# A decoder layer with dilated attention: attention keys stored in three orders, joined loads, and later value and gate products

## The chip, the core and the metric

The kernel runs on one core of a Trainium2 chip. A core has a matrix engine (TensorE, here PE, with its weight loads shown apart as PEld), a vector engine (DVE), a scalar engine (ACT), a third elementwise engine (POOL, also called GpSimd), and an engine (SP) that mostly issues transfers. Sixteen DMA engines move data between DRAM and the on-chip memory of 128 partitions. Matmul results land in PSUM, eight banks of 128 x 512 floats. The metric is the time of one execution on the device in microseconds (us), from the first to the last work of the core; lower is better.

## What is computed

One layer for a sequence of 2048 positions and width 1024, all in float32:

```python
h = rms_norm(x, norm1_g)
q, k, v, u, g = split(h @ w_in)                 # each 512 wide
q, k = rms_norm per head of 64 (8 heads)
a = dilated_attention(q, k, v)                  # branches (window, dilation) = (128,1), (512,4), (2048,16)
m = gelu(u) * (W_s @ layer_norm(gelu(g)) + b)   # chunks of 128 positions, 4 groups, W_s lower triangular
x = x + concat(rms_norm(a), rms_norm(m)) @ w_out
x = x + square(relu(rms_norm(x) @ w_ff1)) @ w_ff2
```

In each attention branch a query at t attends the keys t, t - d, t - 2d, ... down to t - window (d the dilation), that is up to 129 keys among the positions of its residue modulo d. The three branches are combined with weights from their softmax denominators, so a single maximum per query and head over all branches, one sum of exponentials and one weighted sum of values suffice.

## The kernel before

Numbers are split in two parts, a rounded high one and the remainder, so that fast matmuls give float32 accuracy: a product is the sum of high x high, high x low and low x high (`gemm3`, L215; 24 matmuls of 512 columns for a 128 x 512 block of a projection over 1024 inputs). The stages follow one another:

1. **First sweep** (`sweep1`, L340). For each of 16 tiles of 128 positions it computes the q, k and v products (loop L550; c = 0, 1, 2), normalizes q and k, and, one tile behind (`behind`, L509), transposes them to 64 dimensions by positions, two heads to a 128-partition block (`pr` counts the four head pairs), and splits them. Four tiles make a group G. The keys go to DRAM in the order of positions (`kt_d`, L141; `store_t`, L413). The queries go there in the order of their residue modulo 16 (`qt_d`; `store_q`, L420, which first copies each block on ACT (high part) or POOL (low part) and then issues one transfer per half of the partitions). In between, the maxima of branches 1 and 4 are found from the scores of the high parts (`max1`, `max4`, `maxima`, L443 to L492). After the last tile's keys the gate products g of tiles 14 and 15 are made and kept in DRAM (`ge_d`, L578), and then the last maxima. Part of these are done in `finish` (L598), which runs inside the attention's set-up.

2. **Attention** (`attention`, L610). Here every engine's instructions keep the order in which they are written (`InOrder`, L64). For a head, `prepare` (L624) loads `ks` (128 rows: the 64 dimensions' high parts, then their low parts), `qh` (the queries' high part twice), `k2` (the keys' high part and a row of ones, 65 rows) and `q2` (the queries' low part and a row of negated maxima), six transfers of 64 partitions each. The score of a block of 128 keys is then two matmuls with keys as weights:

```python
pe.matmul(ps[:, n : n + w], ks, qh, start=True, stop=False)      # (k high + k low) . q high
pe.matmul(ps[:, n : n + w], k2, q2, start=False, stop=True)      # k high . q low, minus the maximum
```

   A head has 20 jobs: eight for branch 1 (two key blocks each), then for each of four residues r two jobs of branch 4 (two blocks each) and one of branch 16 (four blocks). In branch 1 the keys of a block adjoin; in branch 4 the weights are every fourth key (L831), in branch 16 every sixteenth (L837). A job's scores get the mask added on DVE, two exponentials on ACT (a rounded one and a full one), the difference of the two on POOL (or on DVE, for the jobs in `LODS`), and four jobs later (`PD`) its value matmuls (`pv`, L740; three per block). After the jobs in `MXAT`, four 64-row matmuls and DVE maxima (`group`, L656) find branch 16's maxima for the next head, with its keys at stride 16 as the moving operand. SP issues all loads of the next head at the head's start, values at the jobs `V1AT` and `V4AT`.

3. **Second sweep** (`sweep2`, L923): per tile the products u and g (`gemm_g`, L970, skipped for tiles 14 and 15), the gating (`mixer`, `gate`), the output projection.

4. **MLP** (`mlp`, L1153): by a seven-product scheme of 2 x 2 blocks; the last half of the time.

Outside the attention a scheduler that estimates times orders each engine's instructions, with those written earlier going first among the ones that are ready. Transfers issued by one engine start in the order of its queue, and an instruction that waits holds up those behind it.

Of the kernel before, what the change touches and what calls it, by code (L numbers as in the profile page):

```python
# [8 lines left out]
F32 = mybir.dt.float32  # L9
F32R = mybir.dt.float32r  # L10
# [20 lines left out]
PD, PB, EB, LOL, EVL = 4, 5, 4, 2, 1  # L31
# [4 lines left out]
MXAT = (5, 8, 11, 14)  # L36
V1AT, V4AT = 12, 4
# [3 lines left out]
GEAT = 13  # L41
# [19 lines left out]
PSB, MXB, HS0 = 4, 1, 0  # L61

# [41 lines left out]
def tile_hybrid_block(  # L104
# [35 lines left out]
    qt_d = dram.tile([H, P, S], F32, name="qt_d")  # L140
    kt_d = dram.tile([H, P, S], F32, name="kt_d")  # L141
# [4 lines left out]
    ge_d = dram.tile([2, P, GW], F32, name="ge_d")  # L146
# [169 lines left out]

    mk1 = mkp_pool.tile([P, 2, 256], F32, name="mk1")
# [6 lines left out]
    def masks(m):  # L324

        mk = mkp_pool.tile([P, 384], F32, name=f"mk{m}")
# [7 lines left out]
    m4t, m4e = masks(4)  # L334
    m16t, m16e = masks(16)
# [4 lines left out]
    def sweep1():  # L340
        if True:
# [8 lines left out]
            wh = [zh] + [[wp.tile([P, AW], F32R, name=f"wh{c}_{k}") for k in range(KD)] for c in (1, 2)]  # L350
            wl = [zl] + [[wp.tile([P, AW], F32R, name=f"wl{c}_{k}") for k in range(KD)] for c in (1, 2)]
# [61 lines left out]
            def store_t(dst, part, src, toks):  # L413
                for hh in range(2):
                    nc.sync.dma_start(
                        dst[hh::2, part * HD : (part + 1) * HD, toks].rearrange("h d t -> d h t"),
                        f32(src[hh * HD : (hh + 1) * HD]),
                    )

            def store_q(G):  # L420

                for pr in range(NG):
                    for part, src in ((0, f32(qhis[G])), (1, qlos[G])):
                        src = src[:, pr, :].rearrange("p (i s) -> p s i", s=16)
                        end = G == NT // 4 - 1
                        tag = "qn" if part == 0 and end else "qp"
                        queue = nc.scalar if part == 1 and end else nc.sync
                        qp = sp.tile([P, AW], F32, tag=tag, name="qp", bufs=2).rearrange("p (s i) -> p s i", s=16)
                        if part == 0:
                            nc.scalar.activation(qp, src, AF.Copy)  # L430
                        else:
                            nc.gpsimd.tensor_copy(qp, src)  # L432
                        for hh in range(2):
                            queue.dma_start(
                                qt_d[2 * pr + hh, part * HD : (part + 1) * HD, :].rearrange("d (s i) -> d s i", s=16)[
                                    :, :, G * 32 : (G + 1) * 32
                                ],
                                qp[hh * HD : (hh + 1) * HD],
                            )
# [65 lines left out]
            qhis, qlos = {}, {}  # L505
# [3 lines left out]
            def behind(t, qn, kn, step):  # L509

                G, tg = divmod(t, 4)
                if step == 0:
                    if tg == 0:
                        qhis[G] = sp.tile([P, NG, 512], F32R, tag="qhi", name="qhi")
                        qlos[G] = sp.tile([P, NG, 512], F32, tag="qlo", name="qlo", bufs=1)
                    los["k"] = sp.tile([P, NG, P], F32R, tag="klo", name="klo")
# [4 lines left out]
                    transposed(kn, None, kring[:, :, pos * P : (pos + 1) * P], los["k"])  # L521
                    store_t(kt_d, 1, los["k"], toks)
                    if G == NT // 4 - 1:
                        store_t(kt_d, 0, kring[:, :, pos * P : (pos + 1) * P], toks)
                    elif tg == 3:
                        gt = slice(G * 512, (G + 1) * 512)
                        store_t(kt_d, 0, kring[:, :, (G % 2) * 512 : (G % 2 + 1) * 512], gt)
                    if tg == 3:
                        store_q(G)
# [17 lines left out]

            last = None
            gsrc = w_in[:, 3 * AW + GW : 3 * AW + 2 * GW]
            for t in range(NT):  # L550
# [5 lines left out]
                for c in range(3):  # L556
                    ps = psm.tile([P, AW], F32, tag="mm", name="ps_mm")
# [3 lines left out]
                    if c < 2:  # L561
                        ns.append(normed(ps, r))
                    else:
                        vt = vts[t % 2]
                        split_sb(vt[:, :, 0:HD], vt[:, :, HD + 2 : VW], ps.rearrange("p (h d) -> p h d", d=HD), r)
                        nc.sync.dma_start(v_d[:, t * P : (t + 1) * P, :].rearrange("h t c -> t h c"), f32(vt))
                    if last is not None:
                        behind(t - 1, *last, c)
                    if t == NT - 1 and c == 0:
                        wg["h"], wg["l"] = wg_tiles()  # L570
                        for k in range(KD):
                            raw = sp.tile([P, AW], F32, tag="graw", name="graw", bufs=2)
# [5 lines left out]
            for t in (NT - 2, NT - 1):  # L578
                _, xh, xl, r = xs[t]
                ps = psm.tile([P, AW], F32, tag="mm", name="ps_mm")  # L580
                gemm3(ps, [(xh[:, k, :], xl[:, k, :], wg["h"][k], wg["l"][k]) for k in range(KD)])
                ge = sp.tile([P, GW], F32, tag="graw", name="ge")
                nc.scalar.activation(ge, ps, AF.Copy, scale=r)
                nc.scalar.dma_start(ge_d[t - NT + 2], ge)
# [13 lines left out]
            def finish(pe, dve):  # L598

                order[:] = pe, dve  # L600
                yield lambda pool: load_x_t(pool, pst, 0, nxt=1)
# [8 lines left out]
    def attention(finish, xnp, xs, tpe, wu):  # L610
        with ExitStack() as st:
# [10 lines left out]
            k2s = []  # L622
# [870 lines left out]
```

## Time and profile before

| | |
|---|---|
| median of three runs | 2426.0 us (2423.41 to 2440.55) |
| profiled execution | 2441.18 us, span 2439.5 us |
| PE busy | 2357.1 us (97%) |
| first sweep up to its last keys | 0 to 378 us |
| last products, last maxima, set-up | 378 to 421 us |
| attention | 421 to 731 us |
| second sweep | 731 to about 1190 us |
| MLP | to 2439.5 us |

The profile's groups and timelines give the source line, the engine, the operation, the tiles written and read, and the shapes (for a matmul: weight rows * weight columns, then rows x columns of the moving operand). Lines in attention show as L74, the line of the ordering helper, so they are told apart by tiles: `ps_as` are scores, `ps_o` values, `ps_mx` branch 16's maxima, `ps_sc` the other maxima. Matmuls are pipelined, so their durations overlap and the distance between starts is what one costs. PEclk is the share of TensorE's full clock that was granted.

### The profile page before, as it was taken

Reading aid. Unit: us, or ns where it says so; the run is one execution under the profiler, and the core shown is the slowest. Engines: PE = TensorE matmul, PEld = TensorE weight load, DVE = VectorE, ACT = ScalarE, POOL = GpSimd, SP = SyncE. Lnnn points to the kernel's source line nnn. Section 1 sums busy time; section 2 is a strip of 40 time slices with the busy share of each in tenths; the row PEclk is TensorE's granted clock in tenths of the full one; section 3 lists DMA queues with packets and bytes.
Section 4 is the critical chain, followed back from the end, with each engine's and each line's share of the span. In section 5 each row is a group of like instructions: output and inputs, shape, how many; then the busy total and the mean of one; then the engine's idle time right before and its main releaser. Section 6 shows DMA issues by size and latency. Waiting matters only on the chain. (4 is left out here: it accounts for less than half of the span.)

```text
span 2439.5 us, 31701 instructions
## 1 busy us (share of the span) xinstructions
PE 2357.1 (97%) x11292; PEld 1958.9 (80%) x11292; DVE 1461.1 (60%) x2940; ACT 973.0 (40%) x1584; POOL 843.3 (35%) x657
## 2 busy tenths in 40 slices
PE   8999997999997999998989999999999999999999
PEld 6777775999996788886778887788878888888887
DVE  6556666565565665665775557655557566565542
ACT  5323222656673222223544555555543232222321
POOL 1000001555551122222566666667752001131210
PEclk9999997789898999998999999999999999999999
DMA  6435247656744433333666556654559665575652
GB/s 195 87 79 118 61 101 166 187 150 192 197 148 104 102 89 97 92 89 117 203 191 191 150 154 194 195 155 148 155 177 335 217 198 190 182 241 180 190 172 78
DMA packets 432301, 382.34 MB, mean 157 GB/s; under 512 B 89704, under 2 KB 358632, under 8 KB 427528
## 3 DMA queue, kind: packets, MB, share of 16 engines
q1 hardware_dynamic: 415408, 377.68, 53.1%
q10 hardware_dynamic: 16736, 2.65, 0.7%
q8 instruction: 89, 1.46, 0.3%
q14 instruction: 68, 0.56, 0.1%
HBM read 259.80 MB, written 120.39 MB: 156 GB/s over the span
## 5 line engine op out<-in xcount | busy, mean ns | idle before, releaser
L1292 PE MATMUL ps_f<-hop,wop 128*128 128x512 f32 x2688 | 620.1, 392 | 11.9 <-ACT c L1300 3.2
L1414 PE MATMUL ps_f<-split 128*128 128x512 f32 x2688 | 611.1, 390 | 2.8 <-ACT c L1279 2.8
L1292 PEld LDWEIGHTS ps_f<-hop,wop 128*128 128x128 f32 x2688 | 507.6, 189 | 122.7 <-ACT hop L188 4.3
L1414 PEld LDWEIGHTS ps_f<-split 128*128 128x128 f32 x2688 | 505.8, 188 | 108.2 <-ACT c L1279 3.2
L1204 POOL TENSOR_TENSOR as<-w1r 128x512 f32<-128x512 f32 x160 | 213.5, 1342 | 164.9 <-DVE wop L189 149.6
L188 ACT ACTIVATE split<-sr 128x1024 fp32r<-128x1024 f32 x112 | 118.4, 1060 | 330.5 <-PE ps_f L1414 325.6
L1204 POOL TENSOR_TENSOR c<-c 128x512 f32<-128x512 f32 x160 | 233.7, 1485 | 45.0 <-ACT c L1280 30.7
L1424 DVE TENSOR_TENSOR acc<-acc,ps_f 128x512 f32<-128x512 f32 x192 | 124.4, 682 | 206.1 <-PE ps_f L1414 205.9
L1204 POOL TENSOR_TENSOR raw<-raw 128x1024 f32<-128x1024 f32 x40 | 101.4, 2543 | 420.8 <-DMA raw<-in_w_ff_dram 388.6
L74 POOL TENSOR_TENSOR pl<-e,ph 128x512 fp32r<-128x512 f32 x144 | 175.6, 1231 | 154.8 <-ACT e L74 127.0
L189 DVE TENSOR_TENSOR wop<-as,wop 128x512 fp32r<-128x512 f32 x160 | 149.5, 935 | 91.3 <-ACT wop L188 88.9
L188 ACT ACTIVATE wop<-as 128x512 fp32r<-128x512 f32 x160 | 100.3, 629 | 214.0 <-POOL as L1204 128.0
L74 DVE TENSOR_TENSOR ps_as<-ps_as,mk 128x512 f32<-128x512 f32 (+1 forms) x160 | 105.7, 663 | 122.8 <-PE ps_as L74 112.9
L189 DVE TENSOR_TENSOR split<-sr,split 128x1024 fp32r<-128x1024 f32 x112 | 162.9, 1455 | 16.6 <-ACT split L188 12.0
L74 PE MATMUL ps_o<-ph,v 128*64 128x128 f32 (+3 forms) x816 | 154.0, 276 | 1.4 <-ACT nacc L74 1.4
L74 PE MATMUL ps_as<-qh,ks 128*128 128x256 f32 (+1 forms) x384 | 143.0, 378 | 0.0
L74 ACT ACTIVATE ph<-ps_as 128x512 fp32r<-128x512 f32 (+1 forms) x160 | 92.4, 577 | 126.8 <-DVE ps_as L74 126.6
L432 POOL COPY qp<-qlo 128x512 f32<-128x512 f32 x16 | 17.1, 1074 | 363.5 <-DVE qlo L411 155.3
L74 PE MATMUL ps_as<-q,k 65*128 65x256 f32 (+1 forms) x384 | 139.1, 370 | 0.0
L452 DVE CUSTOM_DVE_ANT_0 jk<-ps_sc,mk 128x256 f32<-128x256 f32 (+1 forms) x232 | 92.5, 399 | 53.3 <-PE ps_sc L448 47.2
L74 PEld LDWEIGHTS ps_o<-ph,v 128*65 128x65 f32 (+1 forms) x816 | 114.4, 157 | 1.6 <-ACT nacc L74 1.6
L74 PEld LDWEIGHTS ps_as<-qh,ks 128*128 128x128 f32 x384 | 108.0, 281 | 3.0
(262 smaller groups left out, 4080.8 us busy)
## 6 DMA issues: line engine op xcount, KB each, us to landing
s_d<-c SPq DMA_DIRECT2D x224, 256.0 KB, 2.2
sr<-s_d SPq DMA_DIRECT2D x112, 512.0 KB, 3.6
raw<-in_w_ff_dram SPq DMA_DIRECT2D x96, 512.0 KB, 4.8
w1r<-in_w_ff_dram SPq DMA_DIRECT2D x128, 256.0 KB, 3.2
v<-v_d SPq DMA_DIRECT2D x24, 1040.0 KB, 12.8
xt<-in_x_dram SPq DMA_DIRECT2D x32, 512.0 KB, 4.1
raw<-h_d SPq DMA_DIRECT2D x28, 512.0 KB, 5.5
v_d<-vt SPq DMA_DIRECT2D x16, 520.0 KB, 6.2
```

What stands on the lines that cost most here:

```text
L74: return self.tc.keep_in_program_order(op(*args, **kwargs))
L188: en.scalar.activation(dst_hi, raw, AF.Copy)
L189: (en.gpsimd if on_pool else en.vector).tensor_tensor(dst_lo, raw, f32(dst_hi), ALU.subtract)
L432: nc.gpsimd.tensor_copy(qp, src)
L452: order[1].tensor_tensor_reduce(jk[:, :n], ps[:, j, :n], mk, 1.0, -3e38, ALU.add, ALU.max, accum_out=m[:, col : col + 1])
L1204: nc.gpsimd.tensor_tensor(dst, a, b, op)
L1292: nc.tensor.matmul(ps[bank], a[:, k, :], b[k], start=first and k == n == 0, stop=(k == 3 and n == 2), skip_group_check=True,)
L1414: nc.tensor.matmul(ps, s[a][:, k, :], t[b][:, k % 2, :], start=k == m == 0, stop=k == NH - 1 and m == 2)
L1424: nc.vector.tensor_tensor(c, c, ps, op)
```

## The change

- **Three orders.** Beside `kt_d` there are now `k4_d` and `k16_d`, the keys ordered by residue modulo 4 and 16, and the queries' `qt_d`; all are laid out by head pair and part (`[NG, 2, P, S]`). `store_g` and `store_by` write them for each group of four tiles: a copy (on POOL, with one exception per order in the last group) and one transfer of 128 partitions. The keys' low parts are kept for four tiles (`klos`) and stored with one transfer a group.
- **Scores.** Branch 4 takes its weights from a tile `k4`, branch 16 from `k16`, both with the keys of a block adjoining. A block's score in these branches is three matmuls (`three`): the row of ones (one weight row) with the negated maxima, the 128 rows with `qh`, and the first 64 rows with the queries' low part. Branch 1 keeps two matmuls, with `k1` and `k2`; there is a single `k2` now. `group` takes its moving operand from `k16`, adjoining.
- **Loads.** `k16`, `k1` and `k4` are one transfer of 128 partitions each, `qh` one with its source repeated. `k4` is loaded at the head's own start, `k1` and `k2` for the next head after job 9 (`K1AT`).
- **Late products.** The value products of tiles 14 and 15 are made after the last tile's keys, and then gate products for four tiles, 14, 15, 12, 13 (`PRE`), the last two with x loaded and transposed once more; the second sweep skips its gate products for these four.
- **Last group.** Only head pair 0 is stored before the attention's set-up; the other 18 blocks are copied and stored in `finish`, through SP's ordered queue.
- **Room.** The masks of branches 4 and 16 are built at the attention's start in a tile that is used again later; `e` has 3 buffers for 4 (`EB`), DVE's share of the differences comes one job earlier (`LOL`), and `MXAT` is (6, 9, 11, 13) for (5, 8, 11, 14).

The core of the diff:

```diff
-PD, PB, EB, LOL, EVL = 4, 5, 4, 2, 1
+PD, PB, EB, LOL, EVL = 4, 5, 3, 1, 1
...
-MXAT = (5, 8, 11, 14)
-V1AT, V4AT = 12, 4
+MXAT = (6, 9, 11, 13)
+V1AT, V4AT, K1AT = 12, 4, 9
...
-GEAT = 13
+PRE = (14, 15, 12, 13)
...
+            def store_by(dst, m, G, pr, part, src, sync):
+
+                end = G == NT // 4 - 1
+                n = 512 // m
+                tag = "qn" if part == 0 and end else "qp"
+                qp = sp.tile([P, AW], F32, tag=tag, name="qp", bufs=2 if tag == "qn" else QPB).rearrange("p (s i) -> p s i", s=m)
+                src = f32(src).rearrange("p (i s) -> p s i", s=m)
+                if end and part == 0 and pr == 0:
+                    nc.scalar.activation(qp, src, AF.Copy)
+                else:
+                    nc.gpsimd.tensor_copy(qp, src)
+                if sync is None:
+                    sync = nc.scalar if part == 1 and end else nc.sync
+                sync.dma_start(dst[pr, part].rearrange("p (s i) -> p s i", s=m)[:, :, G * n : (G + 1) * n], qp)
+
+            def store_g(G, todo, sync=None):
+
+                cols = slice((G % 2) * 512, (G % 2 + 1) * 512)
+                for pr, part in todo:
+                    k, q = (klos[G][:, pr, :], qlos[G][:, pr, :]) if part else (kring[:, pr, cols], qhis[G][:, pr, :])
+                    store_by(qt_d, 16, G, pr, part, q, sync)
+                    store_by(k16_d, 16, G, pr, part, k, sync)
+                    store_by(k4_d, 4, G, pr, part, k, sync)
...
-                        store_q(G)
+                        store_g(G, [(pr, part) for part in (1, 0) for pr in range(NG)] if G < NT // 4 - 1 else ((0, 0), (0, 1)))
...
+                    if c == 2 and t >= NT - 2:
+                        behind(t - 1, *last, c)
+                        continue
...
+                gemm3(ps, [(xh[:, k, :], xl[:, k, :], wh[2][k], wl[2][k]) for k in range(KD)])
+                keep_v(t, ps, r)
+            for n, t in enumerate(PRE):
+                if t < NT - 2:
+                    xs[t] = load_x_t(xp, pst, t, newton=True)
...
-                sy.dma_start(f32(qh[0:HD, :]), qt_d[h, 0:HD, :])
-                sy.dma_start(f32(ks[0:HD, :]), kt_d[h, 0:HD, :])
-                sy.dma_start(f32(ks[HD:P, :]), kt_d[h, HD:P, :])
-                sy.dma_start(f32(q2[0:HD, :]), qt_d[h, HD:P, :])
-                sy.dma_start(f32(qh[HD:P, :]), qt_d[h, 0:HD, :])
-                sy.dma_start(f32(k2[0:HD, :]), kt_d[h, 0:HD, :])
+                both = lambda t: t[pr, :, rows, :]
+                sy.dma_start(f32(k16), both(k16_d))
+                sy.dma_start(f32(qh), qt_d[pr, 0:1, rows, :].broadcast_to([2, HD, S]))
+                sy.dma_start(f32(q2[0:HD, :]), qt_d[pr, 1, rows, :])
...
-                        pe.matmul(ps[:, j, :], qh[0:HD, s * P : (s + 1) * P], ks[0:HD, s::16], start=True, stop=True)
+                        pe.matmul(ps[:, j, :], qh[0:HD, s * P : (s + 1) * P], k16[0:HD, s * P : (s + 1) * P], start=True, stop=True)
...
-                for ks, k2, qh, q2, w in units:
-                    pe.matmul(ps[:, n : n + w], ks, qh, start=True, stop=False)
-                    pe.matmul(ps[:, n : n + w], k2, q2, start=False, stop=True)
+                for pairs, w in units:
+                    for j, (k, q) in enumerate(pairs):
+                        pe.matmul(ps[:, n : n + w], k, q, start=j == 0, stop=j == len(pairs) - 1)
                     n += w
...
+                def three(k, q, q2):
+
+                    return (ones, q2[HD : HD + 1]), (k, q), (k[0:HD], q2[0:HD])
...
-                            s0 = r + cb * 512
-                            kk, qq = slice(s0, s0 + 509, 4), slice(32 * cb, 32 * cb + n)
-                            units.append((ks[:, kk], k2[:, kk], qv[:, r, :, qq], q2v[:, r, :, qq], 4 * n))
+                            kk, qq = slice(512 * r + cb * P, 512 * r + (cb + 1) * P), slice(32 * cb, 32 * cb + n)
+                            units.append((three(k4[:, kk], qv[:, r, :, qq], q2v[:, r, :, qq]), 4 * n))
...
-                        kk, qq = slice(s, None, 16), slice(s * P, (s + 1) * P)
-                        units.append((ks[:, kk], k2[:, kk], qh[:, qq], q2[:, qq], P))
+                        kk = slice(s * P, (s + 1) * P)
+                        units.append((three(k16[:, kk], qh[:, kk], q2[:, kk]), P))
...
-                if t >= NT - 2:
+                if t in PRE:
                     return None
```

`ones` is row 64 of a tile set to 1; the negated maxima lie in row 64 of `q2`.

More of the change, by code (lines that the diff above doesn't have):

```diff
@@ L61 @@
 PSB, MXB, HS0 = 4, 1, 0
+QPB = 3
 class InOrder:
@@ L137, in tile_hybrid_block @@
     dram = ctx.enter_context(tc.tile_pool(name="dram", bufs=1, space=DRAM))
-    qt_d = dram.tile([H, P, S], F32, name="qt_d")
-    kt_d = dram.tile([H, P, S], F32, name="kt_d")
+    qt_d, kt_d, k4_d, k16_d = (dram.tile([NG, 2, P, S], F32, name=f"{n}_d") for n in ("qt", "kt", "k4", "k16"))
     v_d = dram.tile([H, S, VW], F32, name="v_d")
@@ L322, in tile_hybrid_block, with masks @@
     m16f = mk1[:, 0, 0:P].unsqueeze(1).broadcast_to([P, 4, P])
-    def masks(m):
-        mk = mkp_pool.tile([P, 384], F32, name=f"mk{m}")
+    def masks(mk, m):
         nc.gpsimd.memset(mk, 0.0)
@@ L349, in sweep1 @@
             zh, zl = wg_tiles()
-            wh = [zh] + [[wp.tile([P, AW], F32R, name=f"wh{c}_{k}") for k in range(KD)] for c in (1, 2)]
-            wl = [zl] + [[wp.tile([P, AW], F32R, name=f"wl{c}_{k}") for k in range(KD)] for c in (1, 2)]
+            wh, wl = {0: zh}, {0: zl}
+            for w, c in ((wh, 2), (wh, 1), (wl, 1), (wl, 2)):
+                w[c] = [wp.tile([P, AW], F32R, name=f"w{'h' if w is wh else 'l'}{c}_{k}") for k in range(KD)]
             vts = []
@@ L413, in store_t @@
             def store_t(dst, part, src, toks):
[L414 to L439, printed above, removed]
@@ new lines, in store_t @@
+                nc.sync.dma_start(dst[:, part, :, toks].rearrange("g p t -> p g t"), f32(src))
+            def store_by(dst, m, G, pr, part, src, sync):
[11 more added lines that the diff above has]
+                sync.dma_start(dst[pr, part].rearrange("p (s i) -> p s i", s=m)[:, :, G * n : (G + 1) * n], qp)
@@ L546, in late4, with keep_v @@
                     store_m(G, range(H))
+            def keep_v(t, ps, r):
+                vt = vts[t % 2]
+                split_sb(vt[:, :, 0:HD], vt[:, :, HD + 2 : VW], ps.rearrange("p (h d) -> p h d", d=HD), r)
+                nc.sync.dma_start(v_d[:, t * P : (t + 1) * P, :].rearrange("h t c -> t h c"), f32(vt))
             last = None
@@ L596, in sweep1, with finish @@
             st.close()
-            def finish(pe, dve):
+            def finish(pe, dve, sy):
                 order[:] = pe, dve
+                store_g(G, [(pr, part) for pr in range(1, NG) for part in (0, 1)], sy)
                 yield lambda pool: load_x_t(pool, pst, 0, nxt=1)
@@ L641, in prepare, with load_k @@
                 V = {}
-                T = [ks, qh, k2, q2, V]
+                T = [qh, q2, k16, V]
+                def load_k(m):
+                    k = first.pop(m, None)
+                    if k is None:
+                        k = (tp if m == 1 else sp).tile([P, S], F32R, tag=f"k{m}", name=f"k{m}", bufs=1)
+                    T.append(k)
+                    sy.dma_start(f32(k), both(kt_d if m == 1 else k4_d))
+                    if m == 1:
+                        sy.dma_start(f32(k2[0:HD, :]), kt_d[pr, 0, rows, :])
                 def load_v(part):
                     if part == 1:
-                        V[1] = v_tile(tp, "v1")
+                        V[1] = first.pop("v", None)
+                        if V[1] is None:
+                            V[1] = v_tile(tp, "v1")
                         sy.dma_start(f32(V[1]), v_d[h].rearrange("(b i) c -> i b c", i=P))
@@ L692, in due @@
                     f()
-            T, group, load_v = prepare(0)
+            T, group, load_v, load_k = prepare(0)
+            load_k(1)
             load_v(1)
             act.activation(root, ones_c, AF.Exp)
-            more = finish(pe, dve)
+            more = finish(pe, dve, sy)
             if X0S is None:
@@ L905, in attention @@
                         load_now(4)
+                    if h + 1 < H and i == K1AT:
+                        load_k(1)
                     if h + 1 < H and i == V1AT:
```

77 lines of the change are left out of this document (39 added, 38 removed).

## The prediction

> **What bounds the kernel now.** I read the page first, then stretches of the span, then single heads, then the matmuls of two jobs.
>
> ```profile
> PE 2357.1 (97%) x11292; PEld 1958.9 (80%) x11292; DVE 1461.1 (60%) x2940; ACT 973.0 (40%) x1584; POOL 843.3 (35%) x657
> ...
> 0.00:378.00 378.00, 370.46 (x1657) 281.35 (x1658) 232.52 (x898) 125.60 (x236) 19.06 (x34) 1.00 0.45 105
> 391.40:421.10 29.70, 19.66 (x60) 12.66 (x61) 20.10 (x101) 3.57 (x5) 1.80 (x1) 0.50 0.94 206
> 421.10:731.00 309.90, 307.06 (x2127) 299.78 (x2127) 182.87 (x459) 199.11 (x368) 177.47 (x147) 0.85 0.64 176
> 1104.00:1190.00 86.00, 73.71 (x328) 60.39 (x328) 55.55 (x111) 32.84 (x62) 21.28 (x19) 0.92 0.50 162
> ```
>
> The last four rows are stretches: start and end, length, busy time of PE, weight loads, DVE, ACT and POOL, granted clock, DMA share, GB/s. 421.10 to 731.00 is the attention, which the change rewrites. There PE works 307 of 310 us; ACT, the next, 199. So what the change does to PE there sets the result. The clock in that row is 0.85 although PE is never idle.
>
> ```profile
> 421.10:460.50 39.40, 39.40 (x232) 38.27 (x231) 19.52 (x57) 22.62 (x42) 21.61 (x18) 0.68 0.56 147
> 538.50:573.70 35.20, 35.20 (x270) 34.38 (x267) 22.34 (x61) 23.62 (x44) 21.77 (x18) 1.00 0.74 197
> ```
>
> These are heads 0 and 3. The attention's 309.9 us are 38.7 us a head; with the clock at 1.00 one takes 35.2, at 0.68 39.4.
>
> **The scores before.** Start times of consecutive matmuls give the price of each (durations overlap, so I use differences of starts).
>
> ```profile
> 559.78 0.38 PE L74 MATMUL ps_as<-qh,ks 128*128 128x128 f32 x1
> 560.00 0.39 PE L74 MATMUL ps_as<-q,k 65*128 65x128 f32 x1
> ...
> 561.58 0.22 PE L74 MATMUL ps_o<-ph,v 128*64 128x128 f32 x1
> 561.64 0.45 PE L74 MATMUL ps_as<-qh,ks 128*128 128x256 f32 x1
> 561.92 0.40 PE L74 MATMUL ps_as<-q,k 65*128 65x256 f32 x1
> 562.16 0.40 PE L74 MATMUL ps_as<-qh,ks 128*128 128x256 f32 x1
> ...
> 568.11 0.46 PE L74 MATMUL ps_as<-qh,ks 128*128 128x256 f32 x1
> ...
> 573.87 0.29 PE L74 MATMUL ps_as<-q,k 65*128 65x256 f32 x1
> 573.99 0.29 PE L74 MATMUL ps_as<-qh,ks 128*128 128x256 f32 x1
> ...
> 574.24 0.23 PE L74 MATMUL ps_o<-ph,v 128*65 128x128 f32 x1
> 574.31 0.22 PE L74 MATMUL ps_o<-pl,v 128*65 128x128 f32 x1
> ```
>
> With keys at stride 16 as weights a score matmul of 128 columns costs 0.22 us (559.78 to 560.00), at stride 4 one of 256 columns 0.24 (561.92 to 562.16); with adjoining keys 256 columns cost 0.12 (573.87 to 573.99). A value matmul (ps_o) of 128 columns costs 0.06-0.07. So the stride does cost about 0.1 us a matmul, and the change takes it away. The residue period (two jobs of branch 4, one of branch 16, with their value matmuls) runs from 561.64 to 568.11, 6.47 us, and holds one group of the next head's maxima.
>
> **What the change puts in its place.** A unit of branches 4 and 16 was two matmuls, of 128 and of 65 key rows. It becomes three: the one row of ones, 128 rows, 64 rows. The array has shown what a change of row count costs wherever the 64-row maxima (ps_mx) stand between 128-row matmuls:
>
> ```profile
> 563.23 0.22 PE L74 MATMUL ps_o<-pl,v 128*65 128x128 f32 x1
> 563.29 0.22 PE L74 MATMUL ps_o<-ph,v 128*64 128x128 f32 x1
> 563.45 0.69 PE L74 MATMUL ps_mx<-ks,qh 64*128 64x128 f32 x4
> 564.07 0.51 PE L74 MATMUL ps_as<-qh,ks 128*128 128x256 f32 x1
> 564.41 0.40 PE L74 MATMUL ps_as<-q,k 65*128 65x256 f32 x1
> ```
>
> Then the weight loads of the same place, the sixteen maxima that stand alone before head 0, and the group of all maxima (shortest, median and longest in ns):
>
> ```profile
> 563.24 0.14 PEld L74 LDWEIGHTS ps_o<-ph,v 128*64 128x64 f32 x1
> 563.44 0.52 PEld L74 LDWEIGHTS ps_mx<-ks,qh 64*128 64x128 f32 x4
> ...
> 404.35 3.64 PE L74 MATMUL ps_mx<-ks,qh 64*128 64x128 f32 x16 [2.75 <-DMA ks<-kt_d]
> L74 PE MATMUL ps_mx<-ks,qh x128: 285/287/473, 404.4 to 678.8; 64*128 64x128 f32 x128
> ```
>
> The matmul at 563.29 should be followed after 0.06 us; 0.16 passes, and the weight load of the new form starts only then (563.44), not under its predecessor as at 563.24. So a change of form costs a wait of 0.10 and then the whole load in the open. The load of 128 columns is read from the sixteen maxima at half clock: (3.64 - 0.47)/15 = 0.21 us each, so 0.11 at full clock. On the way back 564.07 to 564.41 takes 0.34 where 561.92 to 562.16 takes 0.24. The form of 65 rows costs nothing beside 128 rows, as 573.87 to 573.99 shows; 64 does.
>
> One price is thus wait + load + stream: at full clock 0.10 + 0.11 + 0.12 = 0.33 us for 256 columns, 0.10 + 0.11 + 0.06 = 0.27 for 128. No row shows a matmul of one row of weights. Its bounds: free, if it runs under the 64-row one before it, and the full 0.33 or 0.27. I take the full price, as 64 to 128 and 128 to 64 both pay it, and keep the other as a rival.
> The Trainium skill, "TensorEngine Tiling (Array Packing)", section Tiling Modes, states that changing the tiling mode, not just the tile, drains the array, with 32, 64 and 128 rows as separate modes. By that rule all three matmuls of a unit pay, which is the sum below; the trace agrees for 64 against 128 (0.10 us of wait) and shows no 32.
>
> One residue has 8 units, 24 score matmuls (9 of 256 columns, 15 of 128) and 24 value matmuls of the same sizes. At full clock: 9 x 0.33 + 15 x 0.27 = 7.0; values 9 x 0.12 + 15 x 0.06 = 2.0; three returns to the values, 0.15 each (wait and a 65-column load), 0.45. Sum 9.45 us, against 6.47 less a group. A group costs 563.29 to 564.41 less 0.06 and 0.28 (561.64 to 561.92), 0.78: so 5.7 before.
>
> **The clock.** It falls to half when the array streams too few columns:
>
> ```profile
> 521.10:524.51 3.41, 3.41 (x21) 3.31 (x20) 2.78 (x11) 2.91 (x5) 2.51 (x3) 1.00 0.94 291
> 524.51:527.92 3.41, 3.41 (x23) 3.41 (x23) 1.38 (x2) 2.02 (x3) 1.61 (x2) 0.50 0.74 209
> ```
>
> The 21 matmuls of the first stretch by form are eight rows, the first and the last of them:
>
> ```profile
> L74 PE MATMUL ps_as<-qh,ks 128*128 128x128 f32 x5 | 1.9, 373 | 0.0
> ...
> L74 PE MATMUL ps_as<-q,k 65*128 65x256 f32 x1 | 0.4, 399 | 0.0
> ```
>
> Matmuls at half clock:
>
> ```profile
> 439.69 0.31 PE L74 MATMUL ps_o<-ph,v 128*64 128x128 f32 x1
> 439.93 1.11 PE L74 MATMUL ps_mx<-ks,qh 64*128 64x128 f32 x4
> 440.98 0.60 PE L74 MATMUL ps_as<-qh,ks 128*128 128x256 f32 x1
> 441.37 0.44 PE L74 MATMUL ps_as<-q,k 65*128 65x256 f32 x1
> ...
> 441.98 0.41 PE L74 MATMUL ps_o<-ph,v 128*65 128x256 f32 x1
> 442.19 0.41 PE L74 MATMUL ps_o<-pl,v 128*65 128x256 f32 x1
> ```
>
> The stretch from 521.10 is the last before a fall. Its forms are 9 scores of 128 columns, 2 of 256, 6 values of 256 and a group, 3712 columns, so at most 1090 a microsecond (some only reach into it). Before, a residue with its group streams 7040 + 512 columns in 6.47 us, 1167 a us: just above, which is why the clock wavers between heads. After, it streams 8448 in 9.45 us, 894 a us. I therefore expect half clock through nearly all of each head's part of branches 4 and 16, and recovery in branch 1, whose matmuls follow without gaps.
>
> At half clock the wait is 0.13 (439.69 to 439.93, less 0.11), the load 0.21, the stream 0.21 (441.98 to 442.19) or 0.11: 0.55 and 0.45 us. A residue: 9 x 0.55 + 15 x 0.45 = 11.7, values 9 x 0.21 + 15 x 0.11 = 3.5, returns 3 x 0.24 = 0.7: 15.9 us. Its group costs 439.69 to 441.37, less 0.11 and 0.24: 1.33.
>
> A head after: 4 x 15.9 = 63.6; branch 1 as it is, 35.2 - 4 x 5.7 - 4 x 0.78 = 9.3; groups, one in branch 1 and three behind it, 0.8 + 3 x 1.3 = 4.7. The values run four jobs behind the scores, so the first strided jobs still carry branch 1's dense values and the clock falls late: some 5 us at full clock save 3-4 us, and I take 4. That is 73.6 us, 34.9 more than 38.7; times 8 is 279, less the 2 us by which groups grow, as the last head has none: **+277**.
>
> **The rest of the change.** The 2.75 us wait of PE for ks (row 404.35) goes, as six products now stand between the last keys and it; late next are DVE's maxima, which already pace 391 to 421 (20.10 of 29.70 us busy). Gate products 12 and 13 leave the second sweep and are paid here: the same 24 matmuls each, so nothing; 16 more transposes cost under 2 us. If the products had been cover in 1104 to 1190 (12 us of PE idle there) the move costs up to 11 us; if they fill the 10 idle us of 391 to 421 it gains as much. I take -1.
>
> Matmuls of the first sweep, and the copies that POOL makes there for the queries' low parts:
>
> ```profile
> 358.61 0.39 PE L225 MATMUL ps_mm<-wh,xh 128*128 128x512 f32 x1
> 358.84 0.39 PE L226 MATMUL ps_mm<-wl,xh 128*128 128x512 f32 x1
> ...
> L432 POOL COPY qp<-qlo 128x512 f32<-128x512 f32 x16 | 17.1, 1074 | 363.5 <-DVE qlo L411 155.3 <-DVE qnw L208 131.8 <-DMA qt_d<-qp 76.4
> ```
>
> Three orders need 24 copies on POOL for each 512 positions, 24 x 1.07 = 26 us; the cover is POOL's idleness in the first sweep (19 of 378 us busy) and DMA share 0.45. On SP, the position and value transfers (x, v_d) queue behind 24 stores that wait for those copies; a tile's x is loaded one tile ahead of its use, so if the cover fails it is some 7 us in each of three groups, +20 at most. A gain there is excluded: nothing is taken from PE. In the last group 18 copies and stores and the two masks stand ahead of head 0 on POOL and SP, under the late products, 6 x 24 matmuls of 0.23 us (358.61 to 358.84), 33 us; head 0's first mask add needs them. In attention a head loads 5 MB for 3; at share 0.64 of 38 us, 24 us, plus 2 MB at the 197 GB/s of head 3's row, 10 us: hidden under 74. Three `e` tiles for four cost nothing while ACT has some 24 of 74 us. Sum of the rest: -1, from -10 to +31.
>
> The profiled run took 2441.18 us (span 2439.5), so 2441 + 277 - 1 = 2717; it lies 15 us above the median of the runs shown, 2426.0, from which the forecast is **2702 us**.
>
> **Rivals.**
> *The row of ones is free.* Its row group (64 to 95) is not that of the 64-row matmul before it. Then only the first of each job pays: at half clock 3 + 16 matmuls, 2 x 0.55 + 0.45 + 6 x 0.55 + 10 x 0.45 = 9.4 for 11.7; at full clock still 8448 columns in 0.93 + 4.7 + 2.0 + 0.45 = 8.1 us, 1040 a us, below the falling stretch. 2.3 x 32 = 74 us less: 2628. Against it: both row-count changes seen pay.
> The Trainium skill, "TensorE: Matmul & The Clock Gate", section on packing small matmuls, states that weight loads to other row groups are pulled ahead of running matmuls; by that rule this case holds.
> *The clock holds.* If what the gate counts is not columns, a head is 4 x 9.45 + 9.3 + 3.1 = 50.2, +11.5 x 8 = +92: 2517. For it: I know the threshold from falls alone, and heads such as 3 stay at 1.00.
> *Faster: no wait.* If loads of the new forms go under their predecessors, the price is 0.12 and 0.11 (load-bound): 9 x 0.12 + 15 x 0.11 + 2.0 = 4.7 a residue, 8448 columns in it, clock full; head 31.2, -7.5 x 8 = -60: 2365. It decides where the average surcharge per score matmul of the 96 in a head is under 7.5/96 = 0.08 us. Against it stands 0.10 of wait alone at every ps_mx.
>
> **Chances.** Forecast 0.48 (own range 2660 to 2745: the rest's ends, and 4 us a head either way for when the clock falls and returns); ones free 0.20; clock holds 0.15; faster 0.13; no difference, by a mixture of these, 0.04. About 1% is what a measurement of this kernel tells from no change. Faster 0.13, same 0.04, slower 0.83. The range 2480 to 2745 takes in the three slower cases and leaves out the rest.
>
> **What would show it.** Right: weight loads of the three forms starting 0.1 us after their predecessor's stream, score starts 0.25 us or more apart, PEclk near 0.5 between the branch 1 parts, heads of 65 to 76 us, first and second sweep unchanged. Wrong: score starts 0.11 apart in branch 16, clock 1.00 throughout attention, heads near 31 us; or PE waits on x in the first sweep.

## The result, and the profile after

The changed kernel takes 3175.5 us (median of four runs, 3173.8 to 3181.6) where the kernel before took 2429.0 beside it: a ratio of 1.307, with a 95% interval of 1.302 to 1.312. Slower, as forecast, but 474 us beyond the forecast of 2702 and outside its range. The profiled run took 3173.8 us, its span is 3172.1.

First the page: busy time of PE, then PE and the granted clock in 40 slices.

```profile
PE 2666.6 (84%) x11564; PEld 2125.7 (67%) x11564; DVE 1468.9 (46%) x2954; ACT 970.1 (31%) x1583; POOL 917.6 (29%) x734
...
PE   9999950837638539499899989999899999999999
...
PEclk9999965555555555556999989999999999999999
```

Two things came at once. PE is busy 2667 us for 2357, at half clock through the whole attention, which the prediction had. But PE also stands still there, slices of 0, 3 and 3 among the others, and that it did not have. The stretches (columns as in the prediction) show where the time went:

```profile
0.00:370.00 370.00, 356.52 (x1589) 270.71 (x1590) 240.24 (x862) 114.97 (x226) 78.79 (x84) 0.99 0.62 142
370.00:469.60 99.60, 61.31 (x246) 43.81 (x244) 39.60 (x173) 12.83 (x20) 14.10 (x20) 0.74 0.39 95
469.60:1461.00 991.40, 604.64 (x2352) 458.12 (x2353) 174.96 (x454) 199.00 (x363) 187.85 (x158) 0.54 0.27 76
1461.00:3172.10 1711.10, 1644.08 (x7381) 1353.08 (x7380) 1014.13 (x1467) 643.25 (x976) 636.87 (x472) 0.98 0.53 164
```

Attention begins at 469.6 for 421.1 and lasts 991 us for 310. What follows takes 1711 us; before it was 2439.5 - 731, 1708.5. Of the 991 us PE works 605, close to the 8 x 73.6 = 589 of the forecast. The rest is waiting, and the view of waits (total, times, longest, in us) has it nearly all in one line:

```profile
PE ps_mx L75 <- DMA qh<-qt_d: 382.2, 8, 68.5
PE ps_o L75 <- POOL pl L75: 19.4, 1, 19.4
```

PE stops once ahead of attention (22.9 us) and once in each head but the last, at the first group of the next head's maxima, until that head's `qh` is there: 68.5 us in head 0, 48 to 49 in heads 1 to 6. Head 1 begins at 634.7; its first group by PE's instructions, and SP's issues (start, duration):

```profile
693.74 1.08 PE L75 MATMUL ps_mx<-k,qh 64*128 64x128 f32 x4 [49.33 <-DMA qh<-qt_d]
```

```profile
633.78 0.51 SPq L75 DMA_DIRECT2D k<-k_d  x1
634.34 11.37 SPq L75 DMA_DIRECT2D qh<-qt_d  x1
645.75 19.22 SPq L75 DMA_DIRECT2D q<-qt_d  x1
665.09 15.52 SPq L75 DMA_DIRECT2D v<-v_d  x2
```

What the DMA engines do meanwhile (the last three columns are clock, mean busy share of the 16 DMA engines, GB/s; not all stretches are shown):

```profile
650.00:655.00 5.00, 0.00 (x0) 0.00 (x0) 0.00 (x0) 0.00 (x0) 0.00 (x0) 0.50 0.13 54
655.00:660.00 5.00, 0.00 (x0) 0.00 (x0) 0.00 (x0) 0.00 (x0) 0.00 (x0) 0.50 0.13 54
...
665.00:670.00 5.00, 0.00 (x0) 0.00 (x0) 0.00 (x0) 0.00 (x0) 0.00 (x0) 0.50 0.80 187
...
690.00:693.00 3.00, 0.00 (x0) 0.00 (x0) 0.00 (x0) 0.00 (x0) 0.00 (x0) 0.50 0.12 53
```

PE waits for a transfer, and for most of the wait the transfers run at a share of 0.12 to 0.13: two engines of sixteen, 2/16 = 0.125, at 54 GB/s. The packets say the same: in each of the first two rows 33 packets of 8 KB start and each takes 0.309 us, so 33 x 0.309 / 5 = 2.0 are under way at a time. In between, other loads use nearly all engines for some us, as in the row with 0.80. A joined load is 1.05 MB, so 19.4 us at 54 GB/s. Three of them (`k4`, `k16`, `qh`) come ahead of the group: 58 us when nothing else is under way. The first `k` load of the three is issued at 627.5 and the group starts at 693.7, 66 us later. From the head's start that is 59 us, for 10 of which PE has work. Behind the group PE has 65 us of its own, so a head takes 124.

That suggests theory A: the joined loads, which go over a source of [2, 64, S], run on two engines. Its rivals: the bytes (5 MB for 3), SP's queue, or tiles that the slow matmuls free late.

### The profile page after: what moved, and what is told of

Same layout as the page of the kernel before. It is cut to its first block, busy times and chain, and to the rows that moved or that the text cites. A ratio compares the mean times of both kernels' runs of the same rounds, so it can differ in the third digit from the quotient of the medians.

```text
span 3172.1 us, 32435 instructions
## 1 busy us (share of the span) xinstructions
PE 2666.6 (84%) x11564; PEld 2125.7 (67%) x11564; DVE 1468.9 (46%) x2954; ACT 970.1 (31%) x1583; POOL 917.6 (29%) x734
## 5 line engine op out<-in xcount | busy, mean ns | idle before, releaser
L75 DVE TENSOR_TENSOR ps_as<-ps_as,mks 128x512 f32<-128x512 f32 (+1 forms) x128 | 83.9, 657 | 624.5 <-PE ps_as L75 319.1
L75 PE MATMUL ps_mx<-k,qh 64*128 64x128 f32 x128 | 34.7, 425 | 382.2 <-DMA qh<-qt_d 382.2
L75 PEld LDWEIGHTS ps_mx<-k,qh 64*128 64x128 f32 x128 | 29.4, 321 | 386.7 <-issue 243.9
L75 PE MATMUL ps_o<-ph,v 128*64 128x128 f32 (+3 forms) x816 | 205.7, 339 | 0.0
L75 PE MATMUL ps_as<-qh,k 128*128 128x256 f32 (+1 forms) x384 | 177.6, 466 | 15.2 <-DMA k<-kt_d 8.1
L75 PE MATMUL ps_as<-q,k 64*128 64x128 f32 (+3 forms) x384 | 173.0, 456 | 0.9 <-DMA k<-kt_d 0.9
L75 PEld LDWEIGHTS ps_o<-ph,v 128*65 128x65 f32 (+1 forms) x816 | 145.9, 199 | 13.9 <-issue 7.2
L75 PE MATMUL ps_o<-pl,v 128*65 128x128 f32 (+1 forms) x408 | 134.1, 332 | 19.4 <-POOL pl L75 19.4
```

The lines of the kernel that those rows point to most:

```text
L75: return self.tc.keep_in_program_order(op(*args, **kwargs))
```

## The experiments

**Loads split, all else as changed** (`e1_split`). Each joined load becomes two of 64 partitions (`k1` and `k4` like `k16`):

```diff
-sy.dma_start(f32(k16), both(k16_d))
-sy.dma_start(f32(qh), qt_d[pr, 0:1, rows, :].broadcast_to([2, HD, S]))
+def halves(dst, src):
+    for p in range(2):
+        sy.dma_start(f32(dst[p * HD : (p + 1) * HD, :]), src(p))
+halves(k16, both(k16_d))
+halves(qh, lambda p: qt_d[pr, 0, rows, :])
...
```

> Each of the joined loads of 1 MB (k16, qh, k1, k4) is issued as two transfers of 64 partitions, as the kernel before issued its loads; all else as in the changed kernel. Theory A (a joined load, whose outermost dimension is 2, is carried by two of the 16 DMA engines, and PE waits for it): the 49 us wait of PE at the first group of maxima goes, heads 0 to 6 fall from 124 us to the 74 to 80 us that the last head takes, and part of the 31 us of waits before head 0 goes: 2740 to 2820 us. Rival B (what PE waits for is the number of bytes, 5 MB a head for 3, or SP's queue of issues, not the shape of one transfer): the wait stays and the time stays above 3100 us.

Measured: 2760.0 us, ratio 1.137 (1.134 to 1.140) to the kernel before, within what was expected. Attention and head 3:

```profile
440.80:1041.00 600.20, 572.54 (x2353) 434.66 (x2353) 176.92 (x455) 198.99 (x363) 185.93 (x156) 0.58 0.49 124
689.30:760.20 70.90, 70.90 (x301) 53.88 (x300) 21.75 (x61) 24.16 (x44) 21.64 (x18) 0.60 0.49 127
```

The same bytes, the same queue and more issues, and the wait is gone from this head: PE works all of its 70.9 us. Theory A stands, bytes and queue fall as the cause. Joining the loads costs 3175.5 - 2760.0, some 415 us. Only head 0 still waits for `qh`, once, 16.8 us.

**Joined loads, no change of row count** (`e2_wide_joined`). The maxima's row goes to row `MR` = 96 of `q2`, with zeros in rows 64 to 95, and the matmuls of a unit take 97, 128 and 96 rows:

```diff
...
-queue.dma_start(f32(q2[HD : HD + 1, :]), f32(nm))
+queue.dma_start(f32(q2[MR : MR + 1, :]), f32(nm))
...
-return (ones, q2[HD : HD + 1]), (k, q), (k[0:HD], q2[0:HD])
+return (ones, q2), (k, q), (k[0:MR], q2[0:MR])
```

> The joined loads stay. The score matmuls lose the 64-row and 1-row forms: the maxima's row moves from row 64 to row 96 of q2, rows 64 to 95 of q2 are zero, so that the three matmuls of a unit take 97, 128 and 96 rows; what is computed stays the same. Theory A: the loads are then all that paces a head, about 74 us up to the first group of maxima (3 MB on two engines) and some 25 us behind it, 95 to 105 us a head: 2900 to 3000 us, with PE waiting longer at the group than in the changed kernel. Rival C (the loads come late only because the slow matmuls of the head free their tiles late): without the slow matmuls the wait goes too, and the time is near 2400 us.

Measured: 2972.7 us (one run). Head 3, and the longest of the waits from 400 us on:

```profile
807.50:907.30 99.80, 37.13 (x300) 35.76 (x299) 21.49 (x61) 23.98 (x44) 21.83 (x18) 0.67 0.31 91
```

```profile
PE ps_mx L75 <- DMA qh<-qt_d: 396.8, 8, 61.7
```

PE has only 37 us of work in head 3, and the head still takes 99.8 us, with a wait as long as in the changed kernel (382.2 us in all there). So the loads are not late because the matmuls are slow; the third rival falls.

**Both** (`e3_wide_split`): the two edits above together.

> Both edits together: loads in 64 partitions each, score matmuls of 97, 128 and 96 rows. What is left of the change is adjoining keys with three matmuls for two, three orders of keys and the late products. Theory A with the prediction's price of a change of row count: no such change is left but at the maxima, a head takes 31 to 33 us with the clock near 1.00, attention 250 to 265 us for 310 before; with 20 to 48 us more ahead of it, 2380 to 2430 us. Rival D (forms of 96, 97 and 128 rows are as dear to mix as 64 and 128): score starts 0.25 us apart or more, and 2600 us or more. Rival B: the loads hold it above 2800 us.

Measured: 2491.1 us, ratio 1.025 (1.023 to 1.027): above what was expected. Head 3, the waits, and matmuls of branch 16 at full clock:

```profile
579.50:620.00 40.50, 34.93 (x301) 33.95 (x299) 21.34 (x61) 23.90 (x45) 21.73 (x18) 0.92 0.87 219
```

```profile
PE ps_mx L75 <- DMA qh<-qt_d: 36.7, 7, 10.8
PE ps_o L75 <- POOL pl L75: 15.0, 3, 14.0
```

```profile
600.31 0.28 PE L75 MATMUL ps_as<-qh,k 128*128 128x128 f32 x1
600.42 0.27 PE L75 MATMUL ps_as<-q,k 96*128 96x128 f32 x1
600.53 0.28 PE L75 MATMUL ps_as<-q,ones 97*128 97x128 f32 x1
600.64 0.28 PE L75 MATMUL ps_as<-qh,k 128*128 128x128 f32 x1
```

Forms of 96, 97 and 128 rows mix for nothing: 0.11 us from start to start, the price of a load alone in the prediction, against 0.22 with strided keys before. So the gain that the change aims at is there. It doesn't come out: heads take 38 to 40 us for 35 to 40 before, with the DMA engines busy at 0.87 and PE waiting 3.6 to 4.9 us for `qh` in each of heads 1 to 6. That fits loads that pace the heads even when spread over all engines; `e8_onchip` tries it. The attention of 333 us (440.1 to 773.3) is 23 us longer than before, nearly all of it in head 0 (60 us for 39), and it starts 19 us later.

**Without the row of ones** (`e4_split_no_ones`). The loads are split, and branches 4 and 16 leave the maxima out, so the result is another one:

```diff
-act.activation(ph[:, :n], ps[:, :n], AF.Exp)
+act.activation(ph[:, :n], ps[:, :n], AF.Exp, scale=0.02)
...
-return (ones, q2[HD : HD + 1]), (k, q), (k[0:HD], q2[0:HD])
+return (k, q), (k[0:HD], q2[0:HD])
```

> Loads split as in the first of these, and the one-row matmul of the maxima left out of branches 4 and 16; the exponent's argument is scaled down by 0.02 instead, so the weights of the average are other ones. 128 and 64 rows still alternate. If the one-row matmul costs the full price of a change of row count (0.40 and 0.51 us at half clock, 3 of 256 columns and 5 of 128 in each of four residues and eight heads): 113 us less than the first of these. If it runs under its neighbour for nothing: no less, or 10 us at most.

Measured: 2612.7 us (one run), 147 less than with the loads split alone (`e1_split`). Head 3:

```profile
634.30:688.90 54.60, 54.60 (x269) 44.60 (x269) 21.78 (x61) 24.20 (x44) 21.73 (x18) 0.63 0.66 166
```

16.3 us less a head for the 14.1 expected, and head 0 too is shorter. A matmul with one row of weights pays at least its full price; the rival that it is free falls.

**The price belongs to the change of form** (`e9_split_grouped`). The same matmuls as in `e1_split`, a job's 1-row ones first, then its 128-row and its 64-row ones:

```diff
-for pairs, w in units:
-    for j, (k, q) in enumerate(pairs):
+for j in range(len(units[0][0])):
+    n = 0
+    for pairs, w in units:
+        k, q = pairs[j]
...
```

> As the first of the split kernels (forms of 1, 128 and 64 rows), but a job issues all its one-row matmuls, then all of 128 rows, then all of 64: the same matmuls, three changes of row count a job for three a unit, 9 a residue for 24. If the price belongs to the change: at full clock a residue is 9 x 0.21 for changes, 2.7 for scores at their load or stream, 2.0 for values, 0.45 for returns, 7.1 us, in which 8448 columns pass, 1190 a us, just above the 1167 of the kernel before, so the clock holds for the most part: heads of 41 us for 71, about 2520 us, and up to 2620 if the clock wavers. If the price belongs to matmuls of 1 and 64 rows as such: 2760 us, no change.

Measured: 2637.3 us, ratio 1.083 (1.082 to 1.085), 123 less than `e1_split`. Head 3, and one job of branch 16:

```profile
648.90:705.60 56.70, 56.70 (x301) 48.87 (x300) 21.78 (x60) 24.18 (x44) 21.75 (x18) 0.62 0.63 159
...
688.93 1.11 PE L75 MATMUL ps_as<-q,ones 1*128 1x128 f32 x4
689.97 1.11 PE L75 MATMUL ps_as<-qh,k 128*128 128x128 f32 x4
691.01 1.11 PE L75 MATMUL ps_as<-q,k 64*128 64x128 f32 x4
```

Four of a form take 1.04 us; four with a change ahead of each take 4 x 0.40 = 1.60. The order alone is worth 123 us, so the price belongs to the change. The expected 2520 to 2620 was missed because the clock stayed low, 0.62. It was up as the head's first residue began and fell within it:

```profile
662.50:665.90 3.40, 3.40 (x27) 2.78 (x24) 0.78 (x2) 2.42 (x5) 1.53 (x2) 1.00 1.05 428
665.90:669.30 3.40, 3.40 (x16) 2.88 (x16) 1.79 (x9) 1.51 (x3) 0.00 (x0) 0.60 1.05 308
```

```profile
665.24 0.66 PE L75 MATMUL ps_as<-q,ones 1*128 1x128 f32 x4
665.83 0.66 PE L75 MATMUL ps_as<-qh,k 128*128 128x128 f32 x4
```

The average over a residue, 1190 columns a us, was the wrong measure. One reading is that it hides a slow part: from the maxima ahead of it on, the job of branch 16 has groups of 512 columns at 0.59 us each (two of them are shown), 868 a us. The traces speak for another. In every run the granted clock changes at whole multiples of 3.41 us. Take the columns of the matmuls that start in each such stretch of attention. In the kernel before, the clock falls after stretches of up to 1013 columns a us and stays up in those of 1050 or more; here it falls after stretches of up to 1238. Weight each matmul's columns by its weight rows over 128, and the two kernels nearly agree: it falls after up to 864 before and 901 here, and stays up in stretches of 883 or more before and 921 or more here (one here stays up at 770). So matmuls of 1 and 64 rows seem to count for less towards the clock; no run tests that by itself.

**The joined load in the kernel before** (`e5_before_qh_joined`), and a joined load whose outermost dimension is 128 (`e6_before_ks_joined`):

```diff
-sy.dma_start(f32(qh[0:HD, :]), qt_d[h, 0:HD, :])
+sy.dma_start(f32(qh), qt_d[h : h + 1, 0:HD, :].broadcast_to([2, HD, S]))
...
-sy.dma_start(f32(qh[HD:P, :]), qt_d[h, 0:HD, :])
```

```diff
-sy.dma_start(f32(ks[0:HD, :]), kt_d[h, 0:HD, :])
-sy.dma_start(f32(ks[HD:P, :]), kt_d[h, HD:P, :])
+sy.dma_start(f32(ks), kt_d[h])
```

> The kernel before, with one edit: the two loads of 64 partitions that fill the upper and lower half of qh with the same rows become one load whose source repeats itself twice, as in the changed kernel (the outermost dimension is 2); the bytes that land are the same. Theory A (two engines carry a joined load): 1 MB at the 40 GB/s at which the changed kernel gets 3 MB before its wait ends in 74 us, so 25 us a head on two engines that also carry their share of the rest, some 24 us: heads 0 to 6 go from 38 to 45 to 55 us, PE waits at the first group of maxima for qh, 2480 to 2560 us. Rival B (bytes, or the number of issues): one issue fewer and no byte more, 2429 us within 1%.

> The kernel before, with the two loads of ks joined into one of 1 MB, where the source is 128 adjoining rows of DRAM, so that the outermost dimension is 128. Theory A: sixteen engines carry it as before, no change, 2429 us within 1%. Rival E (any load of 1 MB instead of two of 512 KB comes late, whatever its shape): a wait for ks at the maxima and over 2460 us.

Measured, one run each: 2640.4 us with `qh` joined, 2434.2 with `ks` joined, beside 2435.4 for the kernel before. The loads of `ks` (count, KB each, median us from issue to landing) in the kernel before, with `qh` joined, and with `ks` joined; then the wait with `qh` joined:

```profile
ks<-kt_d SPq DMA_DIRECT2D x16, 512.0 KB, 8.0
```

```profile
ks<-kt_d SPq DMA_DIRECT2D x16, 512.0 KB, 32.9
```

```profile
ks<-kt_d SPq DMA_DIRECT2D x8, 1024.0 KB, 7.2
```

```profile
PE ps_mx L74 <- DMA ks<-kt_d: 197.0, 8, 26.0
```

One joined `qh`, not a byte more, costs 205 us by itself; joining `ks`, of the same size, costs nothing. What differs is the outermost dimension, 2 or 128, and that `qh`'s source repeats its rows. The repeat isn't needed for the slowness: in the changed kernel the share is 0.13 from 650 to 660 as well, where by the order of the queue a `k` load is under way, which repeats nothing. The edit also puts `qh`'s second half ahead of `ks`, but that is 0.5 MB, an estimated 3 us at the 197 GB/s of head 3 before. The time was above the 2560 us expected at most: I had put the slow load beside the rest, but the loads issued behind it come late with it, `ks` by 25 us.

**Two gate products back in the second sweep** (`e7_wide_split_pre2`):

```diff
-PRE = (14, 15, 12, 13)
+PRE = (14, 15)
```

> As the kernel with split loads and forms of 97, 128 and 96 rows, but the gate products of tiles 12 and 13 stay in the second sweep (the list of early ones is 14, 15 as before). If these two products fill no idle time at the first sweep's end and were under other work in the second: 11 us less (2 x 24 x 0.23 us), 2480 us, with the second sweep as long as it was. If the second sweep pays for them: 2491 us, no change. The other 8 us of the later start of attention, and head 0's 60 us, stay in both cases.

Measured: 2479.9 us, ratio 1.019 (1.017 to 1.021), 11.2 less than the kernel with all four (2491.1, ratio 1.025). The part behind attention, with four early products and with two:

```profile
775.60:2485.70 1710.10, 1647.30 (x7359) 1356.18 (x7357) 1011.83 (x1466) 641.35 (x974) 639.57 (x472) 0.98 0.53 164
```

```profile
766.70:2475.70 1709.00, 1653.11 (x7408) 1361.13 (x7405) 1016.35 (x1466) 641.85 (x974) 636.83 (x472) 0.98 0.53 164
```

With 49 matmuls fewer the rest takes as long as with them. So in the second sweep the two products filled time in which PE would have waited; moved ahead, they are paid in full.

**The gain without the transfers** (`e8_onchip`). On the kernel before: keys copied on the chip a residue at a time (behind that residue's scores, for the next head), forms of 97, 128 and 96 rows, nothing else of the change:

```diff
+def in_order(ks, r, e4, e16):
+    ...
+    copy(e4, k4[:, 512 * r : 512 * (r + 1)], f32(ks[:, r::4]))
+    ...
+    src = f32(ks).rearrange("p (i c r) -> p r c i", c=4, r=4)[:, r]
+    copy(e16, k16.rearrange("p (c r i) -> p r c i", c=4, r=4)[:, r], src)
```

> Built on the kernel before (its stores, its loads, its products): what the change is for, without new transfers. Keys at stride 4 and 16 are copied on the chip into two tiles of adjoining keys, a residue at a time, by ScalarE (stride 4) and VectorE (stride 16), one head ahead; the copies of head 0 by GpSimd and ScalarE before it. Branches 4 and 16 take three matmuls of 97, 128 and 96 rows (the maxima's row at row 96, zeros in rows 64 to 95); k2 is loaded once a head into one tile. If the loads were what held the wide and split kernel at 38 to 40 us a head: heads of 32 to 35 us as its last head, 30 to 40 us less in all than the kernel before, 2385 to 2410 us. If the copies, 8 of some 0.6 us a head on engines that wait in order, hold the masks and exponents up: heads of 38 us or more and 2430 us or more.

Measured: 2401.2 us, ratio 0.987 (0.985 to 0.989): faster than both. Attention and head 3:

```profile
421.90:690.60 268.70, 258.07 (x2360) 249.93 (x2361) 209.58 (x481) 223.05 (x393) 179.39 (x144) 0.97 0.73 201
525.40:557.20 31.80, 31.80 (x301) 30.98 (x300) 25.54 (x65) 27.08 (x49) 22.47 (x18) 1.00 0.82 220
```

Attention is 41 us shorter than before (268.7 for 309.9), at a clock of 0.97 for 0.85: adjoining keys also keep the clock up. Heads 1 to 6 take 32 to 33 us, PE doesn't wait for a load in them, and the DMA share of head 3 is 0.82. So what held the wide and split kernel at 38 to 40 us was what this one leaves out; that it was the transfers fits the waits for `qh` there, but the copies and products that go with them were left out together with them.

**Maxima in 128 rows too** (`e10_onchip_max128`), on top of that:

```diff
...
-pe.matmul(ps[:, j, :], qh[0:HD, s * P : (s + 1) * P], ks[0:HD, s::16], ...)
+pe.matmul(ps[:, j, :], qh[:, s * P : (s + 1) * P], ks[:, s::16], ...)
```

> As the kernel with copies on the chip, but the maxima take all 128 rows (high times high plus low times high) for 64, so that no change of row count is left in a head; qh's second half is loaded ahead of ks for it. A group of maxima cost 0.78 us in the kernel before, 0.2 us of it change and open load on the way in and 0.1 to 0.3 on the way back: 0.3 to 0.4 us in each of 28 groups, 8 to 11 us less, 2390 to 2393 us. If the later start of the group (it now needs four loads for three) makes PE wait, or the head is paced by ScalarE and VectorE (223 and 211 of 270 us busy), no gain: 2401 us or more.

Measured: 2440.2 us, ratio 1.002 (1.001 to 1.003): the whole gain is given back.

```profile
537.90:575.30 37.40, 33.26 (x302) 33.15 (x300) 25.47 (x65) 27.31 (x49) 22.68 (x19) 0.91 0.69 186
```

```profile
PE ps_mx L75 <- DMA ks<-kt_d: 28.9, 5, 9.8
```

The group now needs `ks`'s second half, which lands later, and PE waits for it. The clock in head 3 is lower too (0.91 for 1.00).

## Why the prediction was right or wrong

**The stride (right).** 0.22 us a matmul of 128 columns with strided keys, 0.11 with adjoining ones; on the chip, without new transfers, that is worth 41 us of attention.

**Changes of row count (right, a tenth high).** Branch 16 and branch 4 of the changed kernel at half clock, the forecast being 0.45 and 0.55 us a matmul:

```profile
1423.39 0.47 PE L75 MATMUL ps_as<-q,ones 1*128 1x128 f32 x1
1423.79 0.47 PE L75 MATMUL ps_as<-qh,k 128*128 128x128 f32 x1
1424.19 0.47 PE L75 MATMUL ps_as<-q,k 64*128 64x128 f32 x1
1424.60 0.47 PE L75 MATMUL ps_as<-q,ones 1*128 1x128 f32 x1
...
1429.37 0.58 PE L75 MATMUL ps_as<-q,ones 1*128 1x256 f32 x1
1429.88 0.58 PE L75 MATMUL ps_as<-qh,k 128*128 128x256 f32 x1
1430.39 0.58 PE L75 MATMUL ps_as<-q,k 64*128 64x256 f32 x1
```

0.40 and 0.51. The one-row form pays like the others, so the rival of free ones falls, in these rows and by `e4_split_no_ones`. The rival that there is no wait falls too. With the loads split a head takes 70.9 us where 73.6 was forecast. That the 605 us of PE work in the changed kernel lie so near 589 is partly luck: with the loads split it is 572.5. The rest fits matmuls that run at half clock after a wait: from 693.74 to 743.10, right behind one, PE is never idle and the clock is 0.50. The Trainium skill, "TensorEngine Tiling (Array Packing)", section Tiling Modes, has the array drained at a change of mode. The trace agrees as far as it goes: forms of 96 and 97 rows beside 128 cost nothing here, forms of 1 and 64 did.

**The clock (right in what it did, not in what it counts).** 0.54 through attention, where the waits alone keep it at 0.50 for long, and 0.60 in a head with split loads, where PE never waits; the rival that it holds falls. The rule behind the forecast, columns a microsecond, doesn't hold in `e9_split_grouped`, where the clock fell after stretches of up to 1238. It did no harm here, as 894 lies far below either way, and forms of few rows seem to lower the count further.

**The loads (wrong, and this is the error).** The step was: "In attention a head loads 5 MB for 3; at share 0.64 of 38 us, 24 us, plus 2 MB at the 197 GB/s of head 3's row, 10 us: hidden under 74." It took the new loads at the rate of the old ones. Four of the 5 MB come in joined loads, which run on two engines at 54 GB/s, some 19 us each, and three of them in a row stand ahead of the first group of maxima: 59 us from the head's start, in which PE has 10 us to do. That is a wait of 48 to 49 us in each of heads 1 to 6, 68.5 in head 0 and 22.9 ahead of it, and 415 us in the total between `e1_split` and the changed kernel. The joining has no term in the sum, so it was put at nothing without a reason, and no rival had a slow transfer in it. The Trainium skill, "DMA: Bandwidth & Descriptors", section "Why a DMA increments its semaphore by 16 and not by 1", says that the engines of one transfer are the largest number up to 16 that divides the slowest dimension of both sides, and its "Rules for kernel authors" name a leading broadcast as the case to avoid; the share of 0.125 agrees, and so do the two joined loads in the kernel before.

With the loads spread, the size of the term was right: 24 + 10 = 34 us were forecast as share times length, and head 3 of `e3_wide_split` has 0.87 x 40.5 = 35. Under 71 us that is hidden, as forecast; beside matmuls that need 32 to 35 us a head it is not.

**The rest (wrong by its size).** Forecast -1, from -10 to +31. With split loads attention starts 19.7 us later (440.8 for 421.1), and the part behind it is unchanged. Two early gate products are 11 of that (`e7_wide_split_pre2`), the end "If the products had been cover" rather than the middle I took. Most of what is left is a later end of the first sweep, see below. Then head 0 takes 103 us for 71 in `e1_split`: PE waits 16.8 us for `qh`, whose load meets the last group's stores, and 10.9 us for `pl`, as GpSimd's copies hold up the first low parts (19.4 us in the changed kernel). I had put those copies under the late products; they run on into head 0, in the changed kernel to 498.6. With split loads the profiled run took 2750.7 us, 34 above the 2717 forecast for one: 20 of it is the start, 13 attention (600 us for 310 + 277, head 0 longer by 30 and the others shorter). So those 13 us are a sum of errors of opposite sign.

**The first sweep (right on x, too short by 7 us).** PE waits for x once, 4.7 us, as before (4.8), so the stores don't hold up its loads. But the rounding of the last tile's keys (ACT, `kring`) starts at 389.5 for 382.6, although two value products now stand behind it in the program. With the loads split it is 390.0, with two early products 390.2, and 383.0 in `e8_onchip`, which has the old stores and products. Which part of the change costs these 7 us wasn't tried.

## What to carry to other kernels

Read a transfer's access pattern, not its bytes: a joined load whose outermost dimension is 2 ran at 54 GB/s and cost more than the rest of the change together, while two loads of 64 rows, or one of 128 adjoining rows, did not. Keep the row counts of neighbouring matmuls in one form, padding with zero rows if need be, or issue them grouped by form. When a new order of data is wanted and the transfers are near their limit, make it on the chip from what is there already: the idea that lost 31% as written, and 2.5% through DRAM with the loads split and the forms padded, won 1.3% that way.

## What the runs showed that I had not expected

A joined load also holds back what is queued behind it: with `qh` alone joined, `ks` landed after 32.9 us for 8.0, though by theory A fourteen of the engines carry no part of `qh`. The trace of that run shows how. In one head the loads are issued from 628.9 on, and the wait for `ks` ends at 662.5:

```profile
632.00:636.00 4.00, 4.00 (x42) 4.00 (x41) 3.75 (x6) 3.48 (x8) 3.33 (x3) 1.00 1.06 223
648.00:652.00 4.00, 0.00 (x0) 0.00 (x0) 0.00 (x0) 0.00 (x0) 0.00 (x0) 0.50 0.13 55
660.00:662.00 2.00, 0.00 (x0) 0.00 (x0) 0.00 (x0) 0.00 (x0) 0.00 (x0) 0.50 0.14 57
```

At first all engines are busy, then two (but for transfers issued later, between 652 and 657), and PE goes on waiting for `ks`. That fits a `ks` spread over sixteen engines whose parts on two of them stand behind `qh`; the profile doesn't name the engine of a packet. SP's own next issues also took 11 to 19 us while joined loads were under way (645.75 above, 19.22 us). Why the issue takes so long wasn't tried.

A matmul of one row of weights costs as much in this mix as one of 128 rows, 0.40 us at half clock. A matmul of 96 rows, a third of them zeros, costs less than one of 64: 0.11 us from start to start at full clock, where the prediction priced a change of row count at 0.27.
